# HGRN scores within 32 tokens: masked products of 128 sources by 64 targets, or narrow array tiles into compact blocks

## The chip, the cores and the metric

One core of a Trainium2 chip runs the whole kernel in one launch. The metric is the time of one execution on the device, in microseconds (us). TensorE (PE, with its weight loads as PEld), VectorE (DVE), ScalarE (ACT), GpSimd (POOL) and SyncE (SP, which issues the weight DMAs) each run their own instructions in order and wait for each other by semaphores.

## The reference

One decoder layer on 256 tokens of width 2048: an RMSNorm, one input projection of 14864 columns, three causal mixers of width 1024 (HGRN2, RG-LRU, Mamba-2 SSD), and an output projection with gates. The change is in the first mixer alone:

```python
def hgrn2_mixer(q, f_pre, i, lb):            # 8 heads, key and value width 128, chunks of 64 tokens
    log_f = jnp.logaddexp(jnp.log(lbf), jnp.log1p(-lbf) + jax.nn.log_sigmoid(f_pre))
    k = -jnp.expm1(log_f)
    def step(state, inp):
        qb, kb, gb, vb = inp
        b = jnp.cumsum(gb, axis=-2)
        diff = b[:, :, :, None, :] - b[:, :, None, :, :]
        decay = jnp.exp(jnp.where(causal[:, :, None], diff, -jnp.inf))
        scores = jnp.einsum('bhtk,bhsk,bhtsk->bhts', qb, kb, decay)
        o = (jnp.einsum('bhts,bhsv->bhtv', scores, vb)
             + jnp.einsum('bhtk,bhkv->bhtv', qb * jnp.exp(b), state))
        ...
        return state, o
```

The score of target t and source s is a sum over 128 key channels of q(t) k(s) exp(b(t) - b(s)), with a decay of its own in every channel. The kernel needs no state: it makes the scores of all 256 tokens.

## The kernel before

**Projections.** The weights come in blocks, are split by ACT (`whi`, L412) and DVE (`wlo`, L414) into a high and a low part, and are multiplied on TensorE in passes of up to 512 columns (L466 and L467, L519 to L521). These passes fill the array from the first block to the last.

**Mixers between them.** `Streams` holds the mixers as generators that yield between steps. While the program is written, a rough clock of each engine (`Clock`, `Engine.cost`) decides after every few projection passes which steps fit, and their instructions are put into the engines' queues at that place. The order is therefore fixed when the program is built. All mixer instructions are issued through one helper and carry its line, L158, in the profile.

**HGRN scores.** `a_unit(i)` handles two heads (`ct` 0 and 1). Scores of a pair (s, t) are made at the level L (64, 32, 16, 8, 4, 2) at which s lies in the first and t in the second half of the same 2L tokens; there the decay splits in two factors that stay below one, relative to the last token of the first half. So for each level there is a `kl[n]` (sources with their factor) and a row `ql[:, n]` (targets with theirs, only the second halves, packed); `k0` and `q` give the pair of a token with itself and, through the factor `fo`, of an odd token with the one before. `kx` and `ql[:, 6]` give targets 128 to 255 from sources 0 to 127.

Per head and half `j` of 128 tokens the kernel multiplies, for levels 16 to 2, all 128 sources by the 64 packed targets (`p1`, `p2`); `kl` is zero outside first halves, and most of each product is thrown away. The diagonal product is 128 by 192 (`p3`). Levels 64 and 32 have narrower products (64 and 32 output columns). DVE then builds the score tile `sc`: identity times the diagonal, five predicated copies under masks `mk`, three plain copies; ACT copies the cross part. The array multiplies `sc` with the values (`sc,vt`). The PE part of a head is three steps, each with a few projection passes between.

A float32 product is two passes on the array, each with a weight load of its own. In the profile an array tile is given as rows*columns: 128*32 is a product with 32 output columns.

Of the kernel before, what the change touches and what calls it, by code (L numbers as in the profile page):

```python
# [15 lines left out]
P = 128  # L16
# [15 lines left out]
def plan():  # L32
    """The order in which weight blocks are loaded and used."""
# [50 lines left out]
# columns of the per-channel parameters  # L84
# [8 lines left out]
# columns of the constants that depend on shapes alone  # L93
CC = {"ident": (0, 128), "cbm": (128, 384), "scan2": (512, 256), "scan": (128, 512)}
EARLY, LATE, NCC = 768, 128, 768
# [6 lines left out]
class Clock:  # L102
    """Rough times (us) at which the engines are done with what they have been given."""
# [15 lines left out]
class Engine:  # L119
    """An engine whose instructions are timed roughly."""  # L120
# [47 lines left out]
class Streams:  # L168
    """Steps of the mixers, laid between the steps of the projections where their engines have time and their inputs are there.

    A step names the engines that it uses ("p", "a", "v", "g"); all it reads comes from earlier steps."""
# [14 lines left out]
    def room(self):  # L186
        """Waits until a PSUM block is free; its number of readers to come."""
# [5 lines left out]
    def empty(self, gen, n=1):  # L193
        """Adds a stream that reads the last PSUM block, in front of the mixers."""
# [87 lines left out]
def trunk(ctx, tc, xT, xtok, w, wdt, wax, prm, heads, cst, msk, fnw, out):  # L282
# [26 lines left out]
    # the array's clock rises with use: keep it busy until the first weights are there  # L309
# [6 lines left out]
    mk = consts.tile([P, 6, P], U8, name="mk")  # L316
# [14 lines left out]
    # halves that the tanh form of the sigmoid asks for  # L331
# [35 lines left out]
    # the input and the first weights come in by turns  # L367
# [58 lines left out]
    def first_split(u):  # L426
        """Half of the first half tile."""
# [27 lines left out]
    def chan_block(name):  # L455
        """Products into PSUM [128, 2, 512]: two tiles of 128 channels by all tokens, in two parts to add up."""
# [14 lines left out]
    def first_quarter(ps, q, hi, lo, h):  # L471
        """A quarter of the products into PSUM [128, 2, 256]: two tiles of 128 channels by all tokens."""
# [10 lines left out]
    def chan_pair():  # L483
        """The first two blocks, a quarter of each by turns."""
# [22 lines left out]
    def tok_block(name, hi_ap, lo_ap, nk):  # L507
        """Products into two PSUM tiles [128 tokens, 512]."""
# [16 lines left out]
    def last_block(hi_ap, lo_ap, then):  # L525
        """The same for the last block: the first 128 tokens, then half the columns of the others, then the other half."""
# [29 lines left out]
    def chunk(q):  # L556
        """Four tiles of channels of the input in two parts."""
# [43 lines left out]
    def norm_stream():  # L601
        """1 / rms of the tokens, in every partition and per partition."""
# [9 lines left out]
        # one step of Newton's method on what the tables give  # L612
# [22 lines left out]
    def param_stream():  # L635
        # softplus(-lam) = max(-lam, 0) + ln(1 + exp(-|lam|))
# [8 lines left out]
        # lower bound of the forget gate: cumsum over layers of the softmax over layers, minus its first  # L645
# [38 lines left out]
    def joined(o, ps):  # L684
        """The two parts of a block of products, over the rms of their tokens."""
# [5 lines left out]
    def silu2(pool, ps, name):  # L691
        """2 silu(z) of a PSUM block."""
# [750 lines left out]
```

## Time and profile before

| | us |
|---|---|
| median of 3 runs | 860.15 |
| lowest and highest of them | 859.87, 860.79 |
| profiled execution, span from first to last instruction | 858.3 |
| PE busy | 841.2 |
| DVE busy | 638.3 |
| ACT busy | 475.4 |
| POOL busy | 35.0 |
| HGRN groups on the array | 478 to 725 |

The profile shows one execution, and its span is its own time: it is 1.85 us below the median of the runs. A pass on the array is recorded with its whole length through the pipeline (0.39 us for a projection pass of 512 columns), while the next one starts 0.23 us after it; so the spacing of starts tells what a pass costs. In the names, `pmt` is any small PSUM tile, `ql,kl` a level product, `q,k` the diagonal, `ql,kx` the cross product, `ps` a projection, `boh` and `bol` the two parts of a finished mixer output.

### The profile page before, as it was taken

What the parts mean: (1) busy time and instruction counts of PE and PEld (TensorE: products, weight loads), DVE (VectorE), ACT (ScalarE), POOL (GpSimd) and SP (SyncE); (2) the same over time, 40 slices, a digit from 0 to 9 for tenths busy, and PEclk for the clock granted to TensorE, in tenths of its full rate; (3) what the DMA queues carried; (4) which work ended last, traced back from release to release, by engine and by line L of the source; (5) the groups of instructions that cost most, each with busy time, mean ns of one, the idle gap of its engine ahead of it and who ended that gap; (6) DMA issues with size and microseconds to landing.
All of it is one profiled execution on the core that took longest, in us unless ns stands there. A gap on an engine that the chain in (4) does not pass through costs nothing.

```text
span 858.3 us, 11435 instructions
## 1 busy us (share of the span) xinstructions
PE 841.2 (98%) x4441; PEld 715.3 (83%) x4441; DVE 638.3 (74%) x925; ACT 475.4 (55%) x647; POOL 35.0 (4%) x56
## 2 busy tenths in 40 slices
PE   6999999999999999999999999999999999999995
PEld 6888888888888888888888888888888888888885
DVE  7988798777878768678677678778767877666463
ACT  4556455555566736646566367647636754545443
POOL 6310000000000000000100000000000000000000
PEclk9999999999999999999999999999999999999999
DMA  8538455744645455555545435544543554655532
GB/s 297 213 115 284 175 172 196 306 154 148 219 180 208 170 205 189 196 195 177 209 174 196 160 135 197 196 144 151 199 161 131 200 192 148 221 190 185 197 139 99
DMA packets 24646, 159.31 MB, mean 186 GB/s; under 512 B 2816, under 2 KB 3344, under 8 KB 6800
## 3 DMA queue, kind: packets, MB, share of 16 engines
q1 hardware_dynamic: 23072, 151.53, 49.3%
q0 software_dynamic: 1376, 6.96, 2.4%
q8 instruction: 35, 0.57, 0.3%
q10 hardware_dynamic: 144, 0.09, 0.1%
q14 instruction: 19, 0.16, 0.1%
HBM read 156.46 MB, written 2.11 MB: 185 GB/s over the span
## 4 chain that ended last, share of the span: by engine, by line
PE 95%; DVE 2%; DMA 1%; issue 1%; ACT 0%; SPq 0%; POOL 0%; POOLq 0%; DVEq 0%; ACTq 0%
PE ps L466 24%; PE ps L519 17%; PE ps L521 17%; PE ps L520 17%; PE ps L467 12%; PE pmt L158 5%; PE ps L479 1%; DMA raw<-w 1%; DVE wlo L414 1%; DVE hT L158 1%; DVE boh L158 1%; PE pmt L946 1%; PE pmt L748 0%; PE ps L539 0%; PE ps L537 0%
## 5 line engine op out<-in xcount | busy, mean ns | idle before, releaser
L414 DVE TENSOR_TENSOR wlo<-raw,whi 128x1024 fp32r<-128x1024 f32 x275 | 335.7, 1227 | 179.0 <-ACT whi L412 178.6
L412 ACT CAST whi<-raw 128x1024 fp32r<-128x1024 f32 x275 | 288.3, 1051 | 303.1 <-PE ps L521 154.0
L466 PE MATMUL ps<-hT,whi 128*128 128x512 f32 x896 | 318.1, 398 | 0.0
L467 PE MATMUL ps<-hT,wlo 128*128 128x256 f32 x896 | 251.2, 280 | 0.0
L466 PEld LDWEIGHTS ps<-hT,whi 128*128 128x128 f32 x896 | 168.2, 188 | 40.1 <-issue 1.0
L519 PE MATMUL ps<-whi,hT 128*128 128x512 f32 x448 | 175.4, 392 | 0.0
L521 PE MATMUL ps<-whi,hT 128*128 128x512 f32 x448 | 174.5, 390 | 0.0
L520 PE MATMUL ps<-wlo,hT 128*128 128x512 f32 x448 | 174.5, 390 | 0.0
L467 PEld LDWEIGHTS ps<-hT,wlo 128*128 128x128 f32 x896 | 169.3, 189 | 0.4
L521 PEld LDWEIGHTS ps<-whi,hT 128*128 128x128 f32 x448 | 84.1, 188 | 17.7
L519 PEld LDWEIGHTS ps<-whi,hT 128*128 128x128 f32 x448 | 84.1, 188 | 17.2 <-issue 0.3
L520 PEld LDWEIGHTS ps<-wlo,hT 128*128 128x128 f32 x448 | 84.1, 188 | 16.6
L519 PE MATMUL ps<-whi,boh 128*128 128x512 f32 x176 | 69.8, 397 | 0.0
L521 PE MATMUL ps<-whi,bol 128*128 128x512 f32 x176 | 68.6, 390 | 0.0
L520 PE MATMUL ps<-wlo,boh 128*128 128x512 f32 x176 | 68.5, 389 | 0.0
L521 PEld LDWEIGHTS ps<-whi,bol 128*128 128x128 f32 x176 | 33.0, 188 | 6.9
L520 PEld LDWEIGHTS ps<-wlo,boh 128*128 128x128 f32 x176 | 33.1, 188 | 6.3
L519 PEld LDWEIGHTS ps<-whi,boh 128*128 128x128 f32 x176 | 33.1, 188 | 6.2
L131 ACT ACT_TABLE_LOAD x26 | 33.4, 1283 | 1.6 <-PEq L1436 1.2
L479 PE MATMUL ps<-hT,whi 128*128 128x256 f32 x128 | 20.6, 312 | 5.5 <-DVE hT L158 3.0
L479 PEld LDWEIGHTS ps<-hT,whi 128*128 128x128 f32 x128 | 18.3, 213 | 7.1 <-DVE hT L158 3.8
L158 PEld LDWEIGHTS pmt<-ql,kl 128*128 128x128 f32 (+2 forms) x224 | 20.5, 160 | 3.7 <-issue 2.6
(248 smaller groups left out, 709.2 us busy)
## 6 DMA issues: line engine op xcount, KB each, us to landing
raw<-w SPq DMA_DIRECT2D x137, 1024.0 KB, 4.8
raw<-w SPq DMA_DIRECT2D x5, 512.0 KB, 9.9
brd<-sums POOLq DMA_DIRECT2D x4, 512.0 KB, 7.0
xacc<-xtok POOLq DMA_DIRECT2D x1, 2048.0 KB, 12.2
out_dram<-xacc SPq DMA_DIRECT2D x7, 256.0 KB, 2.5
xc_t<-xT SPq DMA_DIRECT2D x3, 512.0 KB, 10.7
wx<-wax POOLq DMA_DIRECT2D x4, 256.0 KB, 3.5
fw<-fnw POOLq DMA_DIRECT2D x1, 1024.0 KB, 7.2
```

The lines of the kernel that those rows point to most:

```text
L131: self.eng.preload_act_table_set(self.set)
L158: return f(*a, **k)
L412: nc.scalar.copy(out=hi, in_=raw[:, sl])
L414: nc.vector.tensor_tensor(out=lo, in0=raw[:, sl], in1=hi.bitcast(F32), op=ALU.subtract)
L466: pe.matmul(ps[:, ct], lhsT=hi[:, c0:c0 + 128], rhs=flat(hT[:, k]), start=k == 0, stop=False)
L467: pe.matmul(ps[:, ct, S:], lhsT=lo[:, c0:c0 + 128], rhs=hT[:, k, 0], start=False, stop=k == KD - 1)
L479: pe.matmul(ps[:, ct], lhsT=(hi, lo)[i][:, c0:c0 + 128], rhs=hT[:, q * 4 + kk, j], start=q == 0 and n == 0, stop=q == 3 and n == last)
L519: pe.matmul(pss[j], lhsT=hi_ap(k, j), rhs=hi[:, sl], start=k == 0, stop=False)
L520: pe.matmul(pss[j], lhsT=hi_ap(k, j), rhs=lo[:, sl], start=False, stop=False)
L521: pe.matmul(pss[j], lhsT=lo_ap(k, j), rhs=hi[:, sl], start=False, stop=k == nk - 1)
L946: pe.matmul(o, lhsT=wp[:, a, ct, g], rhs=xp[:, b, ct], start=u == 0, stop=u == 2)
```

## The change

Within 32 tokens (the diagonal and the levels 16 to 2) sources and targets are multiplied in blocks: 32 sources (one of the four groups `u` of 32 array columns) by the targets of the same 32 tokens: 48 columns for the diagonal, 16 for a level. Four such products, for the four blocks of 128 tokens, write partitions 0, 32, 64 and 96 of one PSUM tile `pd`. `q` is laid out in 16 blocks of 32 tokens with 16 more columns each. DVE builds the diagonal blocks compactly in `dg` (128 x 2 x 32) under masks of 16 columns, and copies them into `sc`, which now are two tiles that stay and whose upper parts POOL clears once. Level 64 is made by two products of 32 columns in place of one of 64. The whole PE part of a head is one step. Comments taken out elsewhere are not shown.

```diff
+CC = {"ident": (0, 128), "cbm": (128, 384), "scan2": (512, 256), "scan": (128, 512), "id32": (640, 32)}
...
-    mk = consts.tile([P, 6, P], U8, name="mk")
+    mk = consts.tile([P, 5, 2, 16], U8, name="mk")
...
-        gp.dma_start(out=cs[:, LATE:LATE + 512], in_=cst[:, EARLY:])
-        mkf = A[1].tile([P, 6, P], F32, tag="ql", name="mkf")
+        gp.dma_start(out=cs[:, LATE:LATE + NLATE], in_=cst[:, EARLY:])
+        mkf = A[1].tile([P, 5, 2, 16], F32, tag="ql", name="mkf")
...
+        A["sc"] = [A[1].tile([P, 3, P], F32, name=f"sc{n}") for n in range(2)]
+        for t in A["sc"]:
+            gp.memset(t, 0.0)
...
         for n, L in enumerate(LEVELS):
-            qv = ql[:, n].rearrange("p (w n l) -> p w n l", w=4, l=L)
-            dve.tensor_tensor(out=qv, in0=qv, in1=q4[:, :, 0:P].rearrange("p w (n two l) -> p w n two l", two=2, l=L)[:, :, :, 1], op=ALU.mult)
...
+            qv = ql[:, n].rearrange("p (w n l) -> p w n l", **g)
+            dve.tensor_tensor(out=qv, in0=qv, in1=to, op=ALU.mult)
...
-        dve.tensor_tensor(out=q4[:, :, P:], in0=q4[:, :, 1:P:2], in1=fo.rearrange("p (w l) -> p w l", w=4), op=ALU.mult)
+        dve.tensor_tensor(out=q[:, :, 32:48], in0=q[:, :, 1:32:2], in1=fo.rearrange("p (w l) -> p w l", w=16), op=ALU.mult)
         yield from st.get("pm", "p")
         op = pm.tile([P, 2, S], F32, name="pmt")
         for ct in range(2):
             h = 2 * i + ct
-            p1 = pm.tile([P, 4, 2, 64], F32, name="pmt")
-            p2 = pm.tile([P, 512], F32, name="pmt")
-            p3 = pm.tile([P, 2, 192], F32, name="pmt")
-            p2v = p2[:, 0:256].rearrange("p (n j u) -> p n j u", n=2, j=2)
-            px = p2[:, 256:384]
+            pf = pm.tile([P, 512], F32, name="pmt")
+            pd = pm.tile([P, 2, 112], F32, name="pmt")
+            far = pf[:, 0:256].rearrange("p (n j u) -> p n j u", n=2, j=2)
+            px = pf[:, 256:384]
+            mm.matmul(px, lhsT=flat(kx[:, ct]), rhs=ql[:, 6, ct * P:(ct + 1) * P], start=True, stop=True)
+
             for j in range(2):
-                ts = slice(ct * S + j * P, ct * S + (j + 1) * P)
-                mm.matmul(p3[:, j], lhsT=k0[:, ts], rhs=q[:, ct, j], start=True, stop=True)
-            for n in (4, 5, 2, 3, 0, 1):
-                for j in range(2):
-                    t0 = ct * S + j * P
-                    qs = ql[:, n, ct * P + j * 64:ct * P + (j + 1) * 64]
-                    if n > 1:
-                        mm.matmul(p1[:, n, j] if n < 4 else p2v[:, n - 4, j], lhsT=kl[n][:, t0:t0 + P], rhs=qs, start=True, stop=True)
-                    elif n == 0:
-                        mm.matmul(p1[0:64, n, j], lhsT=kl[n][:, ct * P + j * 64:ct * P + (j + 1) * 64], rhs=qs, start=True, stop=True)
-                    else:
-                        for u in (0, 1):
-                            mm.matmul(p1[64 * u:64 * u + 32, n, j, 32 * u:32 * u + 32], lhsT=kl[n][:, ct * P + j * 64 + 32 * u:ct * P + j * 64 + 32 * u + 32], rhs=qs[:, 32 * u:32 * u + 32], start=True, stop=True)
-                if n in (5, 3):
-                    yield "p"
-            mm.matmul(px, lhsT=flat(kx[:, ct]), rhs=ql[:, 6, ct * P:(ct + 1) * P], start=True, stop=True)
+                w0 = ct * P + j * 64
+                for u in (0, 1):
+                    mm.matmul(far[32 * u:32 * u + 32, 0, j], lhsT=kl[0][:, w0 + 32 * u:w0 + 32 * u + 32], rhs=ql[:, 0, w0:w0 + 64], start=True, stop=True)
+                for u in (0, 1):
+                    ws = slice(w0 + 32 * u, w0 + 32 * u + 32)
+                    mm.matmul(far[64 * u:64 * u + 32, 1, j, 32 * u:32 * u + 32], lhsT=kl[1][:, ws], rhs=ql[:, 1, ws], start=True, stop=True)
+
+            for j in range(2):
+                t0, w0 = ct * S + j * P, ct * P + j * 64
+                for u in range(4):
+                    mm.matmul(pd[32 * u:32 * u + 32, j, 0:48], lhsT=k0[:, t0 + 32 * u:t0 + 32 * u + 32], rhs=q[:, ct * 8 + j * 4 + u], start=True, stop=True)
+                for n in range(2, 6):
+                    for u in range(4):
+                        mm.matmul(pd[32 * u:32 * u + 32, j, 16 + 16 * n:32 + 16 * n], lhsT=kl[n][:, t0 + 32 * u:t0 + 32 * u + 32], rhs=ql[:, n, w0 + 16 * u:w0 + 16 * u + 16], start=True, stop=True)
             yield "va"
-            sc = a2.tile([P, 3, P], F32, name="sc")
+            sc = A["sc"][ct]
             scd = sc[:, 0:3:2]
-            dve.tensor_tensor(out=scd, in0=p3[:, :, 0:P], in1=ident.unsqueeze(1).broadcast_to([P, 2, P]), op=ALU.mult)
+            dg = a2.tile([P, 2, 32], F32, name="dg")
+            dve.tensor_tensor(out=dg, in0=pd[:, :, 0:32], in1=cc("id32").unsqueeze(1).broadcast_to([P, 2, 32]), op=ALU.mult)
             act.copy(out=sc[:, 1], in_=px)
-            dve.copy_predicated(scd[:, :, 1:P:2], mk[:, 0].rearrange("p (j u) -> p j u", j=2), p3[:, :, P:])
+            dve.copy_predicated(dg[:, :, 1:32:2], mk[:, 0], pd[:, :, 32:48])
...
+            for u in range(0, P, 32):
+                dve.tensor_copy(out=scd[u:u + 32, :, u:u + 32], in_=dg[u:u + 32])
...
-            dve.tensor_tensor(out=o, in0=o, in1=ps[:, :, 0], op=ALU.add)
-            dve.tensor_tensor(out=o, in0=o, in1=r.broadcast_to([P, 2, 2, P]), op=ALU.mult)
+            for c in range(2):
+                dve.tensor_tensor(out=o[:, c], in0=o[:, c], in1=ps[:, c, 0], op=ALU.add)
+            dve.tensor_tensor(out=o, in0=o, in1=r.broadcast_to([P, 2, 8, 32]), op=ALU.mult)
```

How the order of instructions changes is seen at two places. The first is TensorE at the first head (`kl_3683` to `kl_3688` are the levels 64, 32, 16, 8, 4 and 2, `k_3689` is `k0`; a size is output partitions x columns). Before:

```order
L158 MATMUL pmt<-q,k_3689 128x192 x2
L158 MATMUL pmt<-ql,kl_3687 128x64 x2
L158 MATMUL pmt<-ql,kl_3688 128x64 x2
L519 MATMUL ps<-whi,boh 128x512
L520 MATMUL ps<-wlo,boh 128x512
L521 MATMUL ps<-whi,bol 128x512
L158 MATMUL pmt<-ql,kl_3685 128x64 x2
L158 MATMUL pmt<-ql,kl_3686 128x64 x2
L519 MATMUL ps<-whi,boh 128x512
L520 MATMUL ps<-wlo,boh 128x512
L521 MATMUL ps<-whi,bol 128x512
L158 MATMUL pmt<-ql,kl_3683 64x64 x2
```

Four small products of 32x32 and the cross product follow, then 18 projection passes, and then `sc,vt`. TensorE at the same head, as changed:

```order
L158 MATMUL pmt<-ql,kx 128x128
L158 MATMUL pmt<-ql,kl_3683 32x64 x2
L158 MATMUL pmt<-ql,kl_3684 32x32 x2
L158 MATMUL pmt<-ql,kl_3683 32x64 x2
L158 MATMUL pmt<-ql,kl_3684 32x32 x2
L158 MATMUL pmt<-q,k_3689 32x48 x4
L158 MATMUL pmt<-ql,kl_3685 32x16 x4
L158 MATMUL pmt<-ql,kl_3686 32x16 x4
L158 MATMUL pmt<-ql,kl_3687 32x16 x4
L158 MATMUL pmt<-ql,kl_3688 32x16 x4
```

The last five rows come once more for the second 128 tokens; then 15 projection passes stand before `sc,vt`. Three steps have become one, the wide products are gone, and 49 products stand in a row.

The second place is DVE where it builds `sc` for the first head. Before:

```order
L158 TENSOR_TENSOR sc<-pmt,cs 128x2x128
L158 COPY_PREDICATED sc<-mk,pmt 128x2x64
L158 COPY_PREDICATED sc<-mk,pmt 128x2x4x16
L158 COPY_PREDICATED sc<-mk,pmt 128x2x8x8
L158 COPY_PREDICATED sc<-mk,pmt 128x2x16x4
L158 COPY_PREDICATED sc<-mk,pmt 128x2x32x2
L158 COPY sc<-pmt 64x2x64
L158 COPY sc<-pmt 32x2x32 x2
L414 TENSOR_TENSOR wlo<-raw,whi 128x1024 x2
```

DVE at the same place, as changed:

```order
L414 TENSOR_TENSOR wlo<-raw,whi 128x1024 x2
L158 TENSOR_TENSOR dg<-pmt,cs 128x64
L158 COPY_PREDICATED dg<-mk,pmt 128x32
L158 COPY_PREDICATED dg<-mk,pmt 128x2x16
L158 COPY_PREDICATED dg<-mk,pmt 128x4x8
L158 COPY_PREDICATED dg<-mk,pmt 128x8x4
L158 COPY_PREDICATED dg<-mk,pmt 128x16x2
L158 COPY sc_3698<-pmt 64x2x64
L158 COPY sc_3698<-pmt 32x2x32 x2
L158 COPY sc_3698<-dg 32x2x32 x4
L414 TENSOR_TENSOR wlo<-raw,whi 128x1024 x2
```

The same steps work on a quarter of the columns, four copies from `dg` to `sc` come in, and the weight splits (`wlo`) ahead of the chain are two where three stood.

More of the change, by code (lines that the diff above doesn't have):

```diff
@@ L91 @@
 NPC = _n
-CC = {"ident": (0, 128), "cbm": (128, 384), "scan2": (512, 256), "scan": (128, 512)}
-EARLY, LATE, NCC = 768, 128, 768
+CC = {"ident": (0, 128), "cbm": (128, 384), "scan2": (512, 256), "scan": (128, 512), "id32": (640, 32)}
+EARLY, LATE, NLATE, NCC = 768, 128, 544, 768
 SETS = {AF.Exp: ("exp_and_others", "natural_log_exp_and_others"), AF.Ln: ("natural_log_exp_and_others",), AF.Tanh: ("exp_and_others",),
@@ L1136, in a_unit @@
             for n, L in list(enumerate(LEVELS))[2:]:
-                src = p1[:, n] if n < 4 else p2v[:, n - 4]
-                o = scd.rearrange("p j (n two l) -> p j n two l", two=2, l=L)[:, :, :, 1]
-                m = mk[:, n].rearrange("p (j n l) -> p j n l", j=2, l=L)
-                dve.copy_predicated(o, m, src.rearrange("p j (n l) -> p j n l", l=L))
-                if n == 3:
-                    yield "v"
-            dve.tensor_copy(out=scd[0:64, :, 64:P], in_=p1[0:64, 0])
+                o = dg.rearrange("p j (n two l) -> p j n two l", two=2, l=L)[:, :, :, 1]
@@ L1144, in a_unit @@
+                m = mk[:, n - 1].rearrange("p j (n l) -> p j n l", l=L)
+                dve.copy_predicated(o, m, pd[:, :, 16 + 16 * n:32 + 16 * n].rearrange("p j (n l) -> p j n l", l=L))
+            yield "v"
+            dve.tensor_copy(out=scd[0:64, :, 64:P], in_=far[0:64, 0])
             for u in (0, 64):
-                dve.tensor_copy(out=scd[u:u + 32, :, u + 32:u + 64], in_=p1[u:u + 32, 1, :, u // 2:u // 2 + 32])
+                dve.tensor_copy(out=scd[u:u + 32, :, u + 32:u + 64], in_=far[u:u + 32, 1, :, u // 2:u // 2 + 32])
@@ L1192, in copied @@
         if tag == "q":
-            t = pool.tile([P, 2, 2, 192], F32, name=tag, bufs=2)
-            o, ps, r = t[:, :, :, 0:P], ps.rearrange("p c (i j s) -> p c i j s", i=2, j=2), rstd.rearrange("p o (j s) -> p o j s", j=2)
+            t = pool.tile([P, 16, 48], F32, name=tag, bufs=2)
+            o, ps, r = t[:, :, 0:32].rearrange("p (c g) s -> p c g s", c=2), ps.rearrange("p c (i g s) -> p c i g s", i=2, g=8), rstd.rearrange("p o (g s) -> p o g s", g=8)
             for c in range(2):
@@ L1371, in constants @@
     tri = (p[:, None] <= p[None, :])
-    cst = np.zeros((P, EARLY + 512), np.float32)
+    cst = np.zeros((P, EARLY + NLATE), np.float32)
     def put(name, a):
         o, n = CC[name]
-        if name == "scan":
+        if name in ("scan", "id32"):
             o += EARLY - LATE
@@ L1383, in constants @@
     put("scan2", (np.arange(256) % 16 != 0)[None, :])
-    msk = np.zeros((P, 6, 2, 64), np.float32)
-    msk[:, 0] = (p[:, None] == 2 * np.arange(64)[None, :])[:, None, :]
+    put("id32", p[:, None] % 32 == np.arange(32)[None, :])
+    msk = np.zeros((P, 5, 2, 16), np.float32)
+    msk[:, 0] = (p[:, None] % 32 == 2 * np.arange(16)[None, :])[:, None, :]
     for n, L in list(enumerate(LEVELS))[2:]:
-        t = np.arange(P).reshape(-1, 2, L)[:, 1].reshape(-1)
-        ok = (p[:, None] // (2 * L) == t[None, :] // (2 * L)) & (p[:, None] % (2 * L) < L)
-        msk[:, n] = ok[:, None, :]
-    return cst, msk.reshape(P, 6, P)
+        t = np.arange(32).reshape(-1, 2, L)[:, 1].reshape(-1)
+        ok = (p[:, None] % 32 // (2 * L) == t[None, :] // (2 * L)) & (p[:, None] % (2 * L) < L)
+        msk[:, n - 1] = ok[:, None, :]
+    return cst, msk
 def kernel(**inputs):
```

10 lines of the change are left out of this document (8 added, 2 removed).

## The prediction

> **What bounds the kernel now.** I read the page's busy shares and chain first, then stretches of the HGRN stage, then the array's own timeline inside it.
>
> ```profile
> PE 841.2 (98%) x4441; PEld 715.3 (83%) x4441; DVE 638.3 (74%) x925; ACT 475.4 (55%) x647; POOL 35.0 (4%) x56
> PE 95%; DVE 2%; DMA 1%; issue 1%; ACT 0%; SPq 0%; POOL 0%; POOLq 0%; DVEq 0%; ACTq 0%
> core 0: us, PE busy (x) PEld busy (x) DVE busy (x) ACT busy (x) POOL busy (x), PEclk, DMA share, GB/s
> 478.00:560.00 82.00, 82.00 (x466) 70.26 (x465) 61.14 (x99) 45.61 (x68) 0.00 (x0) 1.00 0.47 168
> 560.00:640.00 80.00, 80.00 (x443) 68.68 (x441) 60.47 (x100) 46.12 (x67) 0.00 (x0) 1.00 0.48 170
> 640.00:725.00 85.00, 85.00 (x477) 72.67 (x476) 66.43 (x109) 47.38 (x71) 0.00 (x0) 1.00 0.45 161
> ```
>
> The chain that ends last is TensorE for 95% of the span. In the HGRN stage (478 to 725 us) the array has no idle time at all and full clock, while DVE is busy 188 of 247 us, ACT 139 and POOL none. The array runs one in-order program: projection passes (call them main) with small HGRN groups laid between. So a group is worth what it delays the next main pass, and not its busy time, since a pass's recorded length covers a pipeline that overlaps the next pass. Here is the first head:
>
> ```profile
> 478.56 0.39 PE L521 MATMUL ps<-whi,bol 128*128 128x512 f32 x1
> 478.79 0.81 PE L158 MATMUL pmt<-q,k 128*128 128x192 f32 x4
> 479.43 1.00 PE L158 MATMUL pmt<-ql,kl 128*128 128x64 f32 x8
> 480.24 0.48 PE L519 MATMUL ps<-whi,boh 128*128 128x512 f32 x1
> 480.56 0.40 PE L520 MATMUL ps<-wlo,boh 128*128 128x512 f32 x1
> 480.79 0.40 PE L521 MATMUL ps<-whi,bol 128*128 128x512 f32 x1
> 481.03 1.00 PE L158 MATMUL pmt<-ql,kl 128*128 128x64 f32 x8
> 481.84 0.47 PE L519 MATMUL ps<-whi,boh 128*128 128x512 f32 x1
> 482.15 0.39 PE L520 MATMUL ps<-wlo,boh 128*128 128x512 f32 x1
> 482.38 0.40 PE L521 MATMUL ps<-whi,bol 128*128 128x512 f32 x1
> 482.71 0.69 PE L158 MATMUL pmt<-ql,kl 128*64 128x64 f32 x12
> 483.33 0.49 PE L158 MATMUL pmt<-ql,kx 128*128 128x128 f32 x2
> 483.57 0.48 PE L519 MATMUL ps<-whi,boh 128*128 128x512 f32 x1
> 483.89 0.40 PE L520 MATMUL ps<-wlo,boh 128*128 128x512 f32 x1
> ```
>
> Columns are start, length, engine, line, operation, array tile (rows*columns), moving shape and count. Each float32 product in the program is two passes here, each with its own weight load. Main passes start 0.23 us apart (480.56 to 480.79).
>
> **What goes away.** Three groups per head, each counted from the main pass before it to the second main pass behind it, less two main pitches (0.46), because the first main pass behind a group also starts late (0.32 to its successor in place of 0.23). First: 480.56 - 478.56 - 0.46 = 1.54. Second: 482.15 - 480.79 - 0.46 = 0.90. Third: 483.89 - 482.38 - 0.46 = 1.05. Sum 3.49 us a head, 27.9 us for the eight heads, which repeat these spacings. The group sc,vt (outputs from scores) stays.
>
> **What is added.** One group per head: the cross product kx (2 passes), then 48 products of 32 output columns each, 96 passes, in array tiles 128*32. Of these, 16 passes are the "far" ones (8 with 64 moving columns, 8 with 32), and 80 belong to the compact blocks (16 with 48 moving columns, 64 with 16). The price of a narrow pass comes from the eight that exist now:
>
> ```profile
> 483.08 0.32 PE L158 MATMUL pmt<-ql,kl 128*32 128x32 f32 x8
> L158 PE MATMUL pmt<-ql,kl 128*32 128x32 f32 x64 | 2.5, 201 | 0.0
> 84.94 0.28 PE L467 MATMUL ps<-hT,wlo 128*128 128x256 f32 x1
> 85.15 0.88 PE L158 MATMUL pmt<-ce,xdt 128*64 128x256 f32 x8
> 85.95 0.50 PE L466 MATMUL ps<-hT,whi 128*128 128x512 f32 x1
> ```
>
> Eight passes cover 0.32 us and one alone lasts 0.20, so they start (0.32 - 0.20) / 7 = 17 ns apart. They write partitions 0 to 31 and 64 to 95 in turn, two column groups of the array, so one group takes a pass every 34 ns. That groups really run side by side is seen in the SSD outputs: four passes of 256 and four of 128 moving columns in two halves of the array. A moving column costs 0.84 ns (192 columns in 0.16 us, from 478.79 to 479.43 for four passes), so one after another they would need 4 x 0.215 + 4 x 0.108 = 1.29 us, and main resumes after 0.80.
>
> Working it out for four groups, each at its own pace:
> - kx: 483.33 to 483.57, 0.24.
> - going narrow: main should have ended at 482.38 + 0.23 = 482.61, narrow starts at 482.71, so 0.10, and 0.02 for a first load that nothing covers: 0.12.
> - far passes: the first group has four of 64 columns (0.054 of moving, say 0.058 with the switch) and four at 0.034: 0.37.
> - compact blocks: 20 passes per group, 16 at 0.034 and 4 of 48 columns at 0.045: 0.72.
> - going back: the last narrow pass starts at 483.20 and moves for 0.03, kx starts at 483.33, so 0.10; and a first wide load that nothing covers: 483.33 to 483.89 is 0.56 for kx (0.24) and one main pass (0.23), so 0.09. Together 0.19.
>
> Sum 0.24 + 0.12 + 0.37 + 0.72 + 0.19 = 1.64 us, a saving of 1.85 a head, 14.8 us. The compact passes are the unknown: 80 passes at 8.5 ns (four groups, the value taken, since it is what the measured pace of one group gives and nothing in the rows ties a group to its neighbour), at 17 (what the row shows outright) or slower; the rivals price those.
>
> **What DVE gets.**
>
> ```profile
> 483.50 0.42 DVE L158 TENSOR_TENSOR sc<-pmt,cs 128x256 f32<-128x256 f32 x1
> 484.15 2.00 DVE L158 COPY_PREDICATED sc<-mk,pmt 128x128 f32<-128x128 uint8 x5 [0.23 <-ACT sc L158]
> 486.18 0.65 DVE L158 COPY sc<-pmt 64x128 f32<-64x128 f32 x3
> 487.00 1.23 DVE L414 TENSOR_TENSOR wlo<-raw,whi 128x1024 fp32r<-128x1024 f32 x1 [0.17 <-ACT whi L412]
> L158 DVE COPY rx<-b 128x2 f32<-128x2 f32 x3 | 0.5, 161 | 0.0
> ```
>
> A DVE instruction of 2 elements takes 0.16 us and one of 256 takes 0.42: about 1 ns an element on a floor of 0.16. The identity product drops from 256 to 64 elements, 0.42 to 0.22; five masked copies from 128 to 32 elements, 2.00 to about 1.2; four copies of 64 elements from dg into sc come in, 4 x 0.2 = 0.8; the other three copies stay at 0.65. About 2.9 us against 3.1, and DVE has 59 us free in the stage, so as throughput it is nothing. But sc,vt now waits for that chain from a later start: masks begin only when the whole group is done, and the order has 15 main passes (3.4 us) between group and sc,vt where 18 stood. A chain of 2.9 us leaves 0.5. I take 0.1 us a head, 0.8 in all, between 0 and the price of the DVE rival below. The other edits cost nothing while their cover lasts: POOL's two clears of sc and its smaller mask load fall where POOL idles before the stage (were they late, each would delay the first head alone by less than 1 us); the sum for q in two instructions of 256 columns in place of one of 512 adds one DVE floor of 0.16 a unit, in the same free time; one PSUM block fewer per head, and score tiles kept for good, whose readers of the unit before ended tens of microseconds earlier, add no wait.
>
> **The sum.** 14.8 - 0.8 = 14.0 off the profiled execution's span of 858.3 gives 844.3. The median of the runs, 860.15, is 1.85 above that span; I carry it over: **846 us**.
>
> **Rivals.**
> - *Two at a time* (the groups pair up, or in-order starts hold a product's second pass behind its first and with it all that follows): 80 x 0.017 = 1.36 for the blocks in place of 0.72. Saving 1.85 - 0.64 = 1.21 a head, 9.7 less 0.8: 851. For it: 17 ns is the only narrow pace the trace shows, and never more than two groups were in play. Against: two groups showed no sign of slowing each other.
> - *No overlap*: 96 passes at 34 ns are 3.26, with the 0.55 of fixed parts 3.81, a loss of 0.32 a head: 863, or about 860 if the narrow moves of 16 columns let a pass shrink to 30 ns. Against: both rows above.
> - *Feeding the array* (the slower side). A head's group now is 98 passes and 98 weight loads in a row. The trace's fast runs are short: eight passes at 17 ns. Its other sustained paces are these:
>
> ```profile
> 62.89 0.39 PE L521 MATMUL ps<-whi,hT 128*128 128x512 f32 x1
> 63.21 0.29 PE L158 MATMUL pmt<-cs,dtr 16*128 16x16 f32 x2
> 63.36 0.33 PE L158 MATMUL pmt<-cs,rows 16*128 16x16 f32 x3
> 63.62 0.50 PE L519 MATMUL ps<-whi,hT 128*128 128x512 f32 x1
> 46.52 3.82 PE L748 MATMUL pmt<-hT,wdd 128*48 128x256 f32 x32
> ```
>
> Five transposes with 16 moving columns (0.013 us of moving) ran over 0.33 + 0.15 = 0.48 us; less a last length of 0.21, four steps of 68 ns. 32 passes of L748 started 114 ns apart, which their 256 moving columns (0.215 / 2) nearly explain. If instructions reach the array at no more than one pass per F, the group takes 0.55 + 96 F, and it is as slow as before at F = (3.49 - 0.55) / 96 = 31 ns. At 68 ns: 0.55 + 6.5 = 7.1, a loss of 3.6 a head, 889; at the far end, 114 ns, 924. Against it: eight loads and eight passes were fed at 17 ns per pair, though so few may have stood ready; the transposes may be bound by their 128-column loads.
> [...]
> - *DVE is late*: when the group ends, DVE may have just begun a weight split (1.23 us, row above), ahead of the masks in its queue. The group ends some 1.9 us sooner than it did, so splits that used to fall into it now overhang. 2.9 + 1.23 - 3.4 = 0.7 us of waiting at sc,vt per head, with main passes queued behind it: 5.6 less the 0.8 counted, 851. Against: splits run three blocks ahead, and 0.5 us is free.
> [...]
>
> **Chances.** Four groups abreast 0.46 (846); two at a time 0.18 (851); DVE late 0.10 (851); no overlap 0.10 (860 to 863); feeding 0.16 (884 and up). A measurement of this kernel can tell about 0.2%, 1.7 us. Faster by more: 0.46 + 0.18 + 0.10 = 0.74. Within: half of no overlap, 0.05. Slower: the other half and feeding, 0.21. The range is 843 (a group's pass at 28 ns, no DVE wait: 96 passes then gain 0.2 a head, 1.6, and the 0.8 comes back) to 864, which takes in all but feeding; for the likeliest case alone it is 843 to 849.
>
> **What would show it.** Right: in the timeline the group from kx to the next L519 or L466 covers 1.6 to 1.7 us; the 128*32 passes of a head, 96 in all, start about 11 ns apart on average; the wide groups q,k and ql,kl are gone; TensorE stays busy through the stage. Two at a time: the compact passes start 17 ns apart. Feeding: a steady pitch above 30 ns after the first dozens of passes, the same for 16 and 48 moving columns. DVE: idle of PE before sc,vt, ended by DVE's copies into sc. Wrong altogether: a stage whose main passes no longer start 0.23 us apart, since then something that this trace does not hold has moved.

## The result

The changed kernel takes 846.51 us (median of 4 runs, 846.45 to 848.20) against 860.32 us before (4 runs, 859.87 to 860.79): ratio 0.9845, 95% interval 0.9834 to 0.9857. Run once more in five rounds it took 846.70 against 860.09, ratio 0.9848 (0.9834 to 0.9861). The forecast was 846.

The busy shares and the chain of the profiled execution, in the page of the changed kernel:

```profile
span 846.4 us, 12476 instructions
PE 827.4 (98%) x4953; PEld 702.1 (83%) x4953; DVE 637.3 (75%) x961; ACT 475.2 (56%) x647; POOL 35.9 (4%) x58
PE 95%; DVE 2%; issue 1%; DMA 1%; ACT 0%; POOL 0%; POOLq 0%; SPq 0%; DVEq 0%; ACTq 0%
```

TensorE is as full as before, with 512 more passes in 12 us less. Busy shares cannot show this gain. The first head in TensorE's timeline of the changed kernel can:

```profile
480.03 0.40 PE L521 MATMUL ps<-whi,bol 128*128 128x512 f32 x1
480.27 0.39 PE L158 MATMUL pmt<-ql,kx 128*128 128x128 f32 x2
480.58 0.50 PE L158 MATMUL pmt<-ql,kl 128*32 128x64 f32 x15
480.90 0.24 PE L158 MATMUL pmt<-q,k 128*32 128x48 f32 x3
480.92 0.20 PE L158 MATMUL pmt<-ql,kl 128*32 128x32 f32 x1
480.95 0.25 PE L158 MATMUL pmt<-q,k 128*32 128x48 f32 x5
481.01 0.47 PE L158 MATMUL pmt<-ql,kl 128*32 128x16 f32 x30
...
481.41 0.45 PE L158 MATMUL pmt<-ql,kl 128*32 128x16 f32 x31
481.79 0.50 PE L519 MATMUL ps<-whi,boh 128*128 128x512 f32 x1
482.13 0.40 PE L520 MATMUL ps<-wlo,boh 128*128 128x512 f32 x1
```

Counted as in the prediction, the one group costs 482.13 - 480.03 - 0.46 = 1.64 us, and the same to 0.01 us in all eight heads. The 96 narrow passes start between 480.58 and 481.68 (the last 0.18 before the end of the x31 row): 11.6 ns apart. A far pass of 32 columns (480.92) starts after passes of the next kind (480.90): the column groups do not keep to one common order, nor TensorE as a whole to that of the program.

VectorE's chain of the same head in the timeline, and TensorE's product that waits for it:

```profile
481.92 0.23 DVE L158 TENSOR_TENSOR dg<-pmt,cs 128x64 f32<-128x64 f32 x1 [1.14 <-PE pmt L158]
482.17 1.18 DVE L158 COPY_PREDICATED dg<-mk,pmt 128x32 f32<-128x32 uint8 x5
483.88 0.79 DVE L158 COPY sc<-dg 32x64 f32<-32x64 f32 x4
```
```profile
485.35 0.81 PE L158 MATMUL pmt<-sc,vt 128*128 128x256 f32 x4
```

VectorE idles 1.14 us before the group ends, and is done at 484.67, 0.68 us before sc,vt. There is no wait, nor in the other heads: from 470 to 730 us the view of waits has none on TensorE.

**Where the time went.** Main passes of the two kernels match one to one (3928 in each), so the difference splits exactly. From the start of the HGRN stage to the end, the HGRN groups with the two passes behind each give 14.7 us. All other pairs of main passes together lose 1.3. This execution also entered the stage 1.5 us late, so 11.9 us are left between the two spans, 858.3 and 846.4 (on the late start see after_again below). The loss of 1.3 has one place: the channel blocks, whose passes alternate between L466 and L467. Here nine such pairs in the timelines, first of the kernel before, then of the changed one:

```profile
505.64 0.39 PE L466 MATMUL ps<-hT,whi 128*128 128x512 f32 x1
...
508.76 0.39 PE L466 MATMUL ps<-hT,whi 128*128 128x512 f32 x1
```
```profile
505.62 0.40 PE L466 MATMUL ps<-hT,whi 128*128 128x512 f32 x1
...
508.80 0.40 PE L466 MATMUL ps<-hT,whi 128*128 128x512 f32 x1
```

Nine pairs take 3.12 us before and 3.18 now: three pairs in 1.04 or in 1.06 us, with the same instructions, no idle time and a granted clock of 1.00.

### The profile page after: what moved, and what is told of

The parts are those of the page before. It is cut to its first block, busy times and chain, and to the rows that moved or that the text cites. A ratio compares the mean times of both kernels' runs of the same rounds, so it can differ in the third digit from the quotient of the medians.

```text
span 846.4 us, 12476 instructions
## 1 busy us (share of the span) xinstructions
PE 827.4 (98%) x4953; PEld 702.1 (83%) x4953; DVE 637.3 (75%) x961; ACT 475.2 (56%) x647; POOL 35.9 (4%) x58
## 4 chain that ended last, share of the span: by engine, by line
PE 95%; DVE 2%; issue 1%; DMA 1%; ACT 0%; POOL 0%; POOLq 0%; SPq 0%; DVEq 0%; ACTq 0%
PE ps L466 25%; PE ps L519 17%; PE ps L521 17%; PE ps L520 17%; PE ps L467 12%; PE pmt L158 3%; PE ps L479 2%; DVE wlo L414 1%; PE pmt L946 1%; DVE boh L158 1%; DVE hT L158 1%; DMA xc_t<-xT 1%; PE pmt L748 0%; PE ps L539 0%; PE ps L537 0%
## 5 line engine op out<-in xcount | busy, mean ns | idle before, releaser
L466 PE MATMUL ps<-hT,whi 128*128 128x512 f32 x896 | 318.2, 399 | 0.0
L467 PE MATMUL ps<-hT,wlo 128*128 128x256 f32 x896 | 251.1, 280 | 0.0
L466 PEld LDWEIGHTS ps<-hT,whi 128*128 128x128 f32 x896 | 168.3, 188 | 41.6 <-issue 1.0
L519 PE MATMUL ps<-whi,hT 128*128 128x512 f32 x448 | 175.2, 391 | 0.0
L467 PEld LDWEIGHTS ps<-hT,wlo 128*128 128x128 f32 x896 | 169.1, 189 | 0.5
L519 PEld LDWEIGHTS ps<-whi,hT 128*128 128x128 f32 x448 | 84.1, 188 | 17.4 <-issue 0.3
L519 PE MATMUL ps<-whi,boh 128*128 128x512 f32 x176 | 69.8, 397 | 0.0
L519 PEld LDWEIGHTS ps<-whi,boh 128*128 128x128 f32 x176 | 33.0, 188 | 6.7
L158 ACT ACTIVATE gt<-ps,rtok 128x512 f32<-128x512 f32 x24 | 15.6, 684 | 7.0 <-PE ps L521 6.9
```

Source lines behind the costliest of these rows:

```text
L158: return f(*a, **k)
L466: pe.matmul(ps[:, ct], lhsT=hi[:, c0:c0 + 128], rhs=flat(hT[:, k]), start=k == 0, stop=False)
L467: pe.matmul(ps[:, ct, S:], lhsT=lo[:, c0:c0 + 128], rhs=hT[:, k, 0], start=False, stop=k == KD - 1)
L519: pe.matmul(pss[j], lhsT=hi_ap(k, j), rhs=hi[:, sl], start=k == 0, stop=False)
```

## The experiments

**Is it the column groups, or a common feed?** The changed kernel fits "four groups, each a pass per 34 ns" and also "one feed, a pass per 11.5 ns". Three kernels add the same 80 passes per head, spread over four column groups, two, or one:

```diff
-                for u in range(4):
+                for u in (0, 1, 2, 3, 0, 1, 2, 3):
                     mm.matmul(pd[32 * u:32 * u + 32, j, 0:48], ...)
```

(and the same in the loop over the four short levels; the lines are shortened here; for two groups the list is 0, 1, 2, 3, 0, 1, 0, 1 and for one 0, 1, 2, 3, 0, 0, 0, 0).

> Every compact product is issued twice in a row of four, into the same place (the result stays what it was): 40 products, 80 passes more per head, 20 more on each of the four column groups; all else as in the changed kernel (846.5 us, 1.64 us a group of HGRN passes). Theory, four column groups side by side, each taking a pass every 34 ns (45 with 48 columns): 20 x 0.036 = 0.72 us more per head, a group of 2.36 us, 5.8 us in all, 852.3. Rival, a common feed: the changed kernel's 96 narrow passes start 11.5 ns apart on average; if that is the pace at which instructions come and the column groups have nothing to do with it, 80 x 0.0115 = 0.92 us per head, 7.4 in all, 853.9. Rival, a feed that only short groups escape (the work queued ahead runs out in a longer one): 31 ns or more per added pass, 2.5 us per head, 866 or more.

> The same 80 passes more per head, but all of them on the first two column groups (the products of the first two blocks of 32 sources are issued three times, those of the other two once; the result stays what it was). Theory: the first group now has 40 passes more at 36 ns, 1.44 us per head, a group of 3.08 us, 11.5 in all, 858.0. A common feed: as with four, 0.92 us per head, 853.9, since it is blind to where a pass goes.

> The same 80 passes more per head, all of them on the first column group (the products of the first block are issued five times, the others once; the result stays what it was). Theory: 80 x 0.036 = 2.88 us per head, a group of 4.5 us, 23 in all, 869.5. A common feed: 853.9 as with four and with two.

Measured: 863.73 us (861.65 to 865.84; slower than before, ratio 1.0041, 1.0029 to 1.0053), 866.76 (1.0075, 1.0060 to 1.0090) and 875.83 (1.0178, 1.0163 to 1.0193). By the times alone the column groups would be in doubt: four cost nearly as much as two. The groups' own costs, read as above, say otherwise. Six of the eight heads, in all three kernels, cost:

```
                groups  group, us    more than 1.64   per pass added to the fullest group
twice_four        4     2.34         0.70 (20 passes)    35 ns     (two of the six 2.51 and 2.67)
twice_two         2     2.91         1.27 (40 passes)    32 ns
twice_one         1     4.26         2.62 (80 passes)    33 ns
```

The pace, 32 to 35 ns a pass here, belongs to each column group, and four groups keep it at once. A common feed at 11.5 ns a pass is refuted. The other two heads (the first of units 1 and 3) cost 6.3 to 7.0 us. TensorE's timeline of twice_four in the first of them:

```profile
482.10 0.45 PE L158 MATMUL pmt<-ql,kl 128*32 128x16 f32 x32
486.04 0.62 PE L158 MATMUL pmt<-ql,kl 128*32 128x16 f32 x31 [3.50 <-issue]
486.60 0.80 PE L519 MATMUL ps<-whi,boh 128*128 128x512 f32 x1
487.19 0.63 PE L520 MATMUL ps<-wlo,boh 128*128 128x512 f32 x1
487.62 0.63 PE L521 MATMUL ps<-whi,bol 128*128 128x512 f32 x1
```

In the middle of a run of equal passes the array stops for 3.5 us, and the profile shows nothing that it waits for ("issue"). Then the main passes start 0.43 us apart in place of 0.23. The busy time by stretches shows the granted clock with them (stretch, its length, busy PE, PEld, DVE, ACT and POOL, then the granted clock, the DMA share and GB/s):

```profile
480.00:482.00 2.00, 2.00 (x109) 1.76 (x111) 1.02 (x1) 0.27 (x1) 0.00 (x0) 1.00 0.65 201
486.00:487.00 1.00, 0.96 (x32) 0.92 (x33) 0.24 (x2) 0.00 (x0) 0.00 (x0) 0.50 0.00 0
487.00:489.00 2.00, 2.00 (x6) 1.52 (x6) 1.82 (x10) 0.66 (x1) 0.00 (x0) 0.50 0.03 8
```

So this hole cost its own 3.5 us and then 5 us, 486 to 491, at a granted clock of 0.50 (0.73 in the mean of 491 to 493, 1.00 from 493 to 495). The DMA view of 482.4 to 486.1 us, over the hole, has one packet of a queue named `instruction` among the weights.

```profile
q1 hardware_dynamic: 69, 0.43, 28.5%
q8 instruction: 1, 0.02, 1.6%
```

That queue carried 35 packets in the kernel before, 39 in the changed one and 44 here; in the traces of the first two every packet has 16384 bytes. The differences (4, 5) are those of matmuls and loads over 256: (2 x 512) / 256 and (2 x 640) / 256. Counted whole, the two traces hold 8939 and 9959 TensorE instructions (matmuls, loads, events), 34.9 and 38.9 times 256, for 35 and 39 packets. So these traces have one packet for every 256 TensorE instructions; I call 256 of them a parcel. Counting all instructions of TensorE by their starts, the holes of the whole study, from 450 us on, for which the profile names no awaited engine, lie here (start to start):

```
kernel             hole at, us    length, us    instructions ahead of it    modulo 256
twice_four            482.37         3.68               5313                   193
twice_four            635.20         3.65               8129                   193
twice_two             481.37         3.17               5313                   193
twice_two             634.43         3.32               8129                   193
twice_one             482.15         2.09               5313                   193
twice_one             640.98         2.04               8129                   193
twice_four_moved      560.11         0.46               7105                   193
twice_four_moved      637.32         0.67               8641                   193
twice_four_moved      706.83         0.67               9921                   193
two_heads             692.45         3.25               8641                   193
two_heads_moved       624.42         0.54               7617                   193
two_heads_moved       692.98         3.23               8641                   193
```

Every one stands at the same place modulo 256, 193 (two_heads and the moved kernels follow below); call it a border.

The lengths of the holes go with the time between borders. Each of the eight holes of 2 us and more stands at the second border inside one group, and from the first border to the end of the hole 4.4 to 5.0 us pass in all eight: 481.16 to 486.04 in twice_four, 479.68 to 484.55 in twice_two, 479.36 to 484.24 in twice_one. The longer the passes between take (1.21, 1.69 and 2.79 us), the shorter the hole (3.68, 3.17 and 2.09). That is not a whole rule, since twelve other groups also held two borders, 1.3 to 2.7 us apart, and had no hole or one below 0.7 us; what starts a packet is not shown. In the changed kernel two borders never lie less than 6.4 us apart in the stage.

In six of the 24 groups of 356 narrow instructions in these three kernels a hole of 2.0 to 3.7 us opened.

**Does the hole go when the program is shifted against the parcels?** Sixteen more instructions at the program's start, and nothing else:

```diff
-WARM = 9
+WARM = 13
```

> The kernel that issues every compact product twice (863.7 us, with a hole of 3.7 us in the first head of the first and of the third unit), with one edit at the far end of the program: 13 warm-up products at its start in place of 9, so 16 more TensorE instructions ahead of everything else. Nothing in the HGRN stage is changed. [...] In the two heads with a hole it opens 325 and 333 instructions after the group's start, and in six heads the places fall at other distances (at 313 and 321 there is almost none). With everything 16 instructions earlier, the two become 309 and 317, and none is left: 8 groups of about 2.35 us, 846.5 + 8 x 0.72 = 852, and up to 1 us for the longer warm-up, 852 to 853. Rival, the hole belongs to these two heads or to what other engines and transfers do at that time: it stays, 863.

Measured: 852.73 us (852.49 to 853.04), 11 us faster than the same products without the shift. All eight groups cost 2.34 to 2.35 us but two, with 2.82 and 3.02. The long holes are gone, though the HGRN stage itself is the same, and the doubled kernel comes out near where the theory of the column groups had put it at first (852.3). The distances in the expectation leave out the events ahead of a group; with these, the holes open 295 and 293 instructions after the group's start in place of 325 and 333. That the distance alone decides is not borne out: the two small holes that are left in groups stand at 260 and 258, while borders at 279 and 277 opened nothing.

**Does the order of the products matter?**

```diff
                 for u in range(4):
                     mm.matmul(pd[32 * u:32 * u + 32, j, 0:48], ...)
-                for n in range(2, 6):
-                    for u in range(4):
+                    for n in range(2, 6):
                         mm.matmul(pd[32 * u:32 * u + 32, j, 16 + 16 * n:32 + 16 * n], ...)
```

> The same products as the changed kernel and no more, in another order: for each 128 sources all five products of one block of 32 sources, then the five of the next, so that 10 passes in a row go to one column group (in the changed kernel the target group changes from product to product). [...] If passes can only start in the order of the program, one group works at a time: 34 ns per pass, 80 x 0.036 - 0.72 = 2.2 us more per head, 864. [...]

Measured: 856.50 us (ratio 0.9958, 0.9942 to 0.9974), a group of 2.89 us, between the 846.5 of the changed kernel and the 864 of one group at a time. TensorE's timeline of the first head, by_group:

```profile
479.04 0.25 PE L158 MATMUL pmt<-q,k 128*32 128x48 f32 x2
479.13 0.31 PE L158 MATMUL pmt<-ql,kl 128*32 128x16 f32 x5
479.26 0.23 PE L158 MATMUL pmt<-q,k 128*32 128x48 f32 x1
...
479.50 0.23 PE L158 MATMUL pmt<-q,k 128*32 128x48 f32 x1
```

In one column group, passes of 16 columns start (0.31 - 0.18) / 4 = 32 ns apart, those of 48 columns 0.25 - 0.21 = 0.04 us apart (0.045 by the unrounded starts). A block of ten passes needs 2 x 0.045 + 8 x 0.032 = 0.35 us of its group, and blocks follow at 0.24 us (479.26 to 479.50): the next group starts when the last three or four passes of this one, (0.35 - 0.24) / 0.032, are still to come. So a pass started ahead of others that waited for their group, but here, by this estimate, only some four passes ahead. Three quarters of the gain is lost by the order alone (10 of 13.8 us).

**Was it the narrow tiles, or one group in place of three?** First the changed kernel in three steps again, then the kernel before in one:

```diff
-                for n in range(2, 6):
+                for n in (4, 5):
...
+            yield "p"
+            for j in range(2):
...
+                for n in (2, 3):
...
+            yield "p"
```

```diff
-                if n in (5, 3):
-                    yield "p"
```

> The changed kernel's products, but laid out in three steps per head again with projection passes between them, as before the change: the 48-column products and those of two levels, then two levels, then the far ones and the cross product. Theory, the narrow tiles made the gain and one group in place of three only saves changes of tiling: two more entries and exits per head, 2 x (0.12 + 0.19) = 0.62 us, 5.0 in all, 851.5. Rival, the gain came from drawing three groups into one: most of the 13.8 us are given back, 857 to 860. Rival, entries and exits are covered: 846.5.

> The kernel before, with its wide masked products as they are, but all of a head's products in one step, so in one group. Theory: the wide passes need no change of tiling (only the four narrow products do), so merging saves the exposed weight load behind two groups, 2 x 0.09 us per head, 1.5 us in all, 858.8, and a group of about 3.3 us. Rival, the gain came from drawing three groups into one: 850 or less.

Measured: 850.36 us (ratio 0.9887, 0.9873 to 0.9900) and 861.58 (1.0016, 1.0006 to 1.0025). The first heads in the timelines, three_steps and then before_one_step:

```profile
478.02 0.39 PE L521 MATMUL ps<-whi,bol 128*128 128x512 f32 x1
...
479.25 0.40 PE L520 MATMUL ps<-wlo,boh 128*128 128x512 f32 x1
479.48 0.39 PE L521 MATMUL ps<-whi,bol 128*128 128x512 f32 x1
479.80 0.45 PE L158 MATMUL pmt<-ql,kl 128*32 128x16 f32 x32
...
480.51 0.40 PE L520 MATMUL ps<-wlo,boh 128*128 128x512 f32 x1
480.75 0.39 PE L521 MATMUL ps<-whi,bol 128*128 128x512 f32 x1
...
482.10 0.39 PE L520 MATMUL ps<-wlo,boh 128*128 128x512 f32 x1
```
```profile
478.82 0.39 PE L521 MATMUL ps<-whi,bol 128*128 128x512 f32 x1
479.05 0.81 PE L158 MATMUL pmt<-q,k 128*128 128x192 f32 x4
479.70 2.52 PE L158 MATMUL pmt<-ql,kl 128*128 128x64 f32 x28
...
482.70 0.39 PE L520 MATMUL ps<-wlo,boh 128*128 128x512 f32 x1
```

Three narrow steps cost 0.77 + 0.57 + 0.89 = 2.23 us a head, 0.59 over one (forecast 0.62). One wide step costs 482.70 - 478.82 - 0.46 = 3.42, against 3.49 in three: the wide passes have the array tile of the main passes, 128*128, and one step in place of three saved 0.07 us, less than the 0.18 that I had. (That kernel's channel blocks also fell into the slower rhythm, 245 of 261 stretches; so it gained nothing.) Of the 14.7 us in the groups 10 come from the narrow tiles alone, and one group in place of three gives 4.7, but only once the tiles are narrow.

**How far is VectorE from the path?**

```diff
+            for _ in range(6):
+                nc.vector.tensor_tensor(out=dg, in0=pd[:, :, 0:32], in1=cc("id32")..., op=ALU.mult)
```

> The changed kernel with its first VectorE instruction on the scores (the product with the identity, 0.23 us) issued seven times in place of once, so that the chain from the group's end to the scores ends six of them, about 1.5 us, later; the result stays what it was and the planner is told nothing, so the order of the projections is the same. In the changed kernel's trace the last copy into the scores ends at 484.67 and the product that reads it starts at 485.35: 0.68 us free. Theory: TensorE waits 1.5 - 0.7 = 0.8 us per head, 6.5 in all, 853, and the waits stand before sc,vt. If the chain was already the limit in some heads (the 0.1 us per head of the prediction): up to 1.5 us per head, 858. If sc,vt had more room than the row shows: 846.5.

Measured: 853.42 us (ratio 0.9922, 0.9908 to 0.9935), and among the waits of 470 to 730 us a new one:

```profile
PE pmt L158 <- DVE sc L158: 6.7, 8, 0.9
```

Eight waits, as forecast. What they cost is seen in the timeline of the first head, VectorE and then TensorE:

```profile
479.97 1.52 DVE L1144 TENSOR_TENSOR dg<-pmt,cs 128x64 f32<-128x64 f32 x6 [1.14 <-PE pmt L158]
481.52 0.23 DVE L158 TENSOR_TENSOR dg<-pmt,cs 128x64 f32<-128x64 f32 x1
...
483.48 0.79 DVE L158 COPY sc<-dg 32x64 f32<-32x64 f32 x4
```
```profile
483.17 0.39 PE L521 MATMUL ps<-whi,bol 128*128 128x512 f32 x1
484.41 0.89 PE L158 MATMUL pmt<-sc,vt 128*128 128x256 f32 x4 [0.85 <-DVE sc L158]
```

The last copy ends at 484.27, and sc,vt starts 0.14 us behind it. Without a wait it would have started at 483.17 + 0.23 = 483.40, so it is 1.01 us late. The six products took 1.55 us; so of the 0.68 us in the changed kernel only 0.54 were free, and the other 0.14 is the way from the copy to sc,vt. VectorE's work cost nothing there, and costs at once beyond 0.54 us. Over the eight heads the groups and the passes behind them take 8.6 us longer than in the changed kernel, and not the 6.5 of the forecast; the 6.7 us of the row hold only the time in which the array is idle. That the total still came out at 853 is luck: this kernel's channel blocks ran in the faster rhythm (255 of 261 stretches), which gave 1.8 us back.

**Two ways to go further.** The first spreads the far products evenly:

```diff
-mm.matmul(far[64 * u:64 * u + 32, 1, j, 32 * u:32 * u + 32], ...)
+mm.matmul(far[64 + 32 * u:96 + 32 * u, 1, j, 32 * u:32 * u + 32], ...)
...
```

(VectorE's copies read from the new places.)

> The changed kernel with one edit: the far products of the level of 32 tokens go to the third and fourth column groups, where they went to the first and third; VectorE's copies fetch them from there. The first column group then has four far passes of 64 columns, where it had these and four of 32. Theory, the far part ends with the first column group: 4 x 0.058 = 0.23 in place of 0.37 us, 0.14 less per head, 1.1 in all, 845.4 where the changed kernel has 846.5. Rival, the far passes are paced by something else (their loads, or the order of the program): no difference.

Measured: 845.59 us (845.49 to 845.83; ratio to before 0.9831, 0.9818 to 0.9844), and in its timeline

```profile
478.39 0.40 PE L521 MATMUL ps<-whi,bol 128*128 128x512 f32 x1
...
480.37 0.39 PE L520 MATMUL ps<-wlo,boh 128*128 128x512 f32 x1
```

a group of 480.37 - 478.39 - 0.46 = 1.52 us: 0.12 less per head. It is the fastest kernel of the study. Its interval overlaps that of the changed kernel (the two were not timed together), but eight times 0.12 us is the 0.9 us between the medians.

The second puts both heads of a unit into one group, on top of the first (and once more with `WARM = 11`):

```diff
         for ct in range(2):
-            h = 2 * i + ct
-            pf = pm.tile([P, 512], F32, name="pmt")
-            pd = pm.tile([P, 2, 112], F32, name="pmt")
...
+            mm.matmul(pxs[:, ct], lhsT=flat(kx[:, ct]), ...)
+        for ct in range(2):
+            far = pf[:, ct].rearrange("p (n j u) -> p n j u", n=2, j=2)
...
+        for ct in range(2):
+            pd = pds[:, ct]
...
+        for ct in range(2):
+            h = 2 * i + ct
...
             yield "va"
```

> The kernel with the far products spread (845.6 us, 1.52 us a group), with both heads of a unit in one group: the two cross products, then all far ones, then all compact ones; 196 passes and 196 loads in a row. The scores of both heads are then made one after the other, before the two products that read them. Theory on the tiling alone: one entry and one exit per unit are saved, 0.31 us, 1.2 us in all, 844.4; a group of 2 x 1.52 - 0.31 = 2.73 us. Theory with the parcels of instructions: 392 instructions in a row; counted from the group's start the second parcel's border lies at 325 in the first unit (a hole, some 3 us and then some 2 us of slower clock), at 265 in the second, and in the third and fourth behind the group's end: one hole, 849 to 850. If every such group ran dry: 844.4 + 4 x 5.5, 866.

> The same with 11 warm-up products at the program's start in place of 9, 8 TensorE instructions more. Theory with the parcels: the borders move 8 instructions forward, the first unit's to 317, where no hole or a small one was seen, and the fourth unit's still lies behind its group's end: 844 to 845. If holes have another cause: as without the move.

Measured: 847.48 us (846.00 to 848.39) and 847.80 (846.27 to 848.82). Three of the four groups cost 2.67 us, where the theory on the tiling alone gave 2.73; the fourth had a hole. (The forecast for one hole was 849 to 850; the channel blocks of two_heads ran mostly in the faster rhythm, 208 of 261 stretches, which gave 1.4 us back.) In two_heads:

```profile
692.36 0.28 PE L158 MATMUL pmt<-ql,kl 128*32 128x16 f32 x12
695.70 0.36 PE L158 MATMUL pmt<-ql,kl 128*32 128x16 f32 x19 [3.07 <-issue]
```

One hole, as forecast, but in another unit: I had placed the borders without counting events; with them the fourth unit has one at 356 instructions (348 in the moved kernel, so the move could not help), and it opened there. In the first unit a border at 295 opened nothing, where twice_four had its hole at 295 from the same start. So the distance alone does not decide. The traces differ in when a packet of the `instruction` queue came: at 478.01 us here, ahead of the group, and at 483.85 in twice_four, where the queue moved none from 480 to 482.4 while weights kept the DMA engines 75% busy. Whether such a transfer is what delays it was not tried.

**What belongs to the program, and what to one execution?**

> The changed kernel once more, unedited, for two questions that one profiled execution leaves open. First, its HGRN stage began 1.5 us later than that of the kernel before (480.0 against 478.6), and the execution with that profile took 848.2 us where the other three took 846.5. If that belongs to the execution, the stage begins near 478.4 here and the span is 844.8; if it belongs to the program, it begins near 480.0 again. Second, its channel blocks run in the HGRN stage with 1.06 us for three pairs of passes (257 of 261 such stretches), where the kernel before mostly took 1.04 (195 of 249). If the rhythm belongs to the program, 257 or so again; if it is drawn anew by each execution, some other share, and the time moves by up to 1.7 us with it.

Measured: 846.70 us, span 844.5. The timeline of this execution:

```profile
478.14 0.40 PE L521 MATMUL ps<-whi,bol 128*128 128x512 f32 x1
...
480.24 0.40 PE L520 MATMUL ps<-wlo,boh 128*128 128x512 f32 x1
```

The late start of 480.0 belonged to that one execution: it entered the stage 1.9 us later than this one, which is the whole difference of the two spans (846.4 and 844.5) and accounts for its 848.2 us. What delayed it ahead of the stage was not looked into. The group costs the same 1.64. And 258 of 261 stretches of three pairs again take 1.06 us: the rhythm belongs to the program.

## Why the prediction was right

- **What goes away**, 3.49 us a head: it went.
- **What is added**, 1.64: measured 1.64. (From kx to the next L519 alone it is 1.52 us, 480.27 to 481.79, and not the 1.6 to 1.7 named as a sign: 0.1 of the cost shows only behind that L519, as the prediction's own working has it.) The step on which it stood, that four column groups run side by side at the pace measured for one, is shown by the three kernels with 80 passes more: 32 to 35 ns per pass of the fullest group, however many groups are in play. Of its terms, the far passes are 0.37 only as long as one group holds eight of the sixteen (far_spread: 0.12 less), and going narrow and back is 0.30 (three_steps: 0.59 for two more of each).
- **What DVE gets**: the chain was put at 2.9 us with 0.5 free; it took 2.75, with 0.68 to the start of sc,vt, of which dve_later shows 0.54 to be free. The 0.1 us a head that I charged for lateness was mis-sized: it measured 0, so 0.8 us of the sum were not spent.
- **The sum**: 14.8 - 0.8 = 14.0. Measured, from 858.3 to the 844.5 of after_again: 14.7 in the groups, no VectorE wait, 1.3 lost in the channel blocks' rhythm, on which the prediction had no term, and 0.4 gained ahead of the stage; 13.8 in all. Small errors of opposite sign hid each other: the mechanism was right, but that the time came within 0.5 us of the forecast is luck. The last of its signs of being wrong, main passes with another spacing, had come true in a small way. In the range, the lower end gives a head 0.2 us for passes at 28 ns; the 24 passes of the fullest group, 6 ns less each, give 0.14.
- **Rivals.** Two at a time: refuted by 9.9 ns per compact pass here (80 between 480.90 and 481.68) where it needed 17, and by 80 more passes that cost 0.70 us on four column groups and 1.27 on two. Its mechanism, a pass that holds up those behind it, is seen in by_group beyond some four passes, at a price (856.5). No overlap: refuted by twice_one, whose 80 passes on one group cost 2.62 us against 0.70 on four. DVE late: refuted by the 0.68 us and by the waits, of which there are none; dve_later shows what it would have cost. Feeding: the steady pitch that it needs is not there (32 and 45 ns in one group, by columns; 11.6 over all narrow passes of a head). No run shows a pace behind the 884 us that stand with its chance of 0.16: the 96 passes of a head and their loads ran at 11.6 ns a pass. Yet these traces show stops of another kind, at borders 256 instructions apart. A head's group has 196 and meets at most one border; the doubled groups of 356 could hold two, and the shift by 16 instructions shows that their holes cost some 11 us (863.73 to 852.73).

## What to carry to other kernels

Where small float32 products start further apart than their moving columns explain (here passes of 128*128 with 64 columns, (1.00 - 0.27) / 7 = 0.10 us apart by the row at 479.43 in the prediction, where 64 columns at 0.84 ns are 0.054), try narrow tiles on all four column groups and let the program change the group with each product; by these runs the cost is passes of the fullest group times 32 ns (45 at 48 moving columns), plus 0.3 us for going narrow and back. Keep a run of short TensorE instructions below 256, counting loads, so that it cannot hold two places 256 apart: here runs of 196 never stopped, some of 356 and 392 did, and no length between was tried. Judge such a group by the delay of the pass behind it and VectorE by its free time, never by busy shares.

## What was not expected of the hardware

- TensorE stopped in the middle of a run, and the profile names no engine that it waited for: holes of 2.0 to 3.7 us, all at 193 modulo 256 and at the second border of a run, 4.4 to 5.0 us from the first border to their end; in the doubled kernel they were gone after a shift by 16 instructions. What decides whether one opens stayed open.
- The granted clock was 0.50 after such holes: from 486 to 491 us in twice_four (hole 3.68 us), from 484 to 490 in twice_one (2.09 us).
- The same alternating passes run in one of two rhythms, 1.04 or 1.06 us for three pairs, steady over whole blocks and the same in two executions of one program. In the HGRN stage 195 of 249 stretches were fast in the kernel before, 1 of 261 in the changed one, 255 of 261 in dve_later. What picks the rhythm was not found; it was worth 1.3 us here.
- A narrow pass costs its column group 32 ns with 16 moving columns (by_group) and hardly more, 34, with 32 (the row of the kernel before in the prediction); with 48 it is some 45. So at 16 columns, 13 ns at 0.84 ns each, it is not the columns that set the pace.
